# Linear attention on one Trainium2 core: log decays split into two rounded parts, running sums from rounded products

## The chip, the cores and the metric

The kernel runs on one core of one Trainium2 chip. The metric is device time in microseconds of one execution, as the median of several runs. The engines of the core are named as the profile names them: PE (TensorE matmul; PEld is its weight load), DVE (VectorE), ACT (ScalarE), POOL (GpSimd) and SP (SyncE, which issues DMAs).

## What is computed

The kernel is a two-layer backbone over 2048 latent and 256 context tokens of width 1024. The change concerns one part of the first layer, the bidirectional gated linear attention: 4 heads, key width 64, value width 128. Cut to what matters, the reference computes per direction:

```python
logits = jnp.einsum('bnzr,zrk->bnzk', r, gate_w) + gate_b
g = jax.nn.log_sigmoid(logits.astype(jnp.float32)) / GATE_TAU      # log decays
...
b = jnp.cumsum(gi, axis=-2)                                         # running sums in a chunk
b_last = b[..., -1:, :]
q_t = qi * jnp.exp(b)
k_t = ki * jnp.exp(-b)
att = jnp.where(mask, jnp.einsum('bhld,bhmd->bhlm', q_t, k_t), 0.0)
o = jnp.einsum('bhld,bhde->bhle', q_t, state) + jnp.einsum('bhlm,bhme->bhle', att, vi)
k_dec = ki * jnp.exp(b_last - b)
state = state * jnp.exp(b_last)[..., 0, :, None] + jnp.einsum('bhld,bhle->bhde', k_dec, vi)
```

All inputs are float32.

## The kernel before

The kernel goes through both layers in stages; the linear attention belongs to the stage `even_mix`, in which the latent attention (`even_attention`, heads in four pairs) is the main stream of PE and the linear attention (`gla`) is woven into it. The 2304 tokens are cut into 18 chunks of 128, and each chunk holds both directions side by side: a tile of 128 tokens x 512 columns is 4 heads x 2 directions x 64.

Per chunk, in `gla`:

- `logits` (L725): one rounded product of the low-rank gate gives 128x512 logits in PSUM; DVE makes G = min(logit, 0) (L733) and e = 2G - logit (L734), two tiles of 512 floats.
- `softplus` (L737): ACT makes e = ln(1 + exp(e)) in two passes (they are booked under the helper's line L106), then POOL makes G = G - e (L744). G is the log decay, still without the factor 1/16.
- `decays` (L752): PE makes `mid`, the running sums within a half chunk, as two products of a triangular 128x128 matrix `tri` with G (L759, one per direction, 256 columns), and `hs`, the sums over half chunks, as four products with G as weights and the two-column matrix `ind` (L763). Both are float32 products. ACT takes exponentials of hs into `fac` and of mid into `gqt` and `gkt` (L106); POOL multiplies two columns of fac (L768); DVE multiplies gqt and gkt by the queries and keys (L773).
- `within` (L790): PE forms scores (L799), DVE masks them (L802, two tiles, "gat" and "ge"), POOL adds the two (L804).
- `values` and `added` (L808, L818): PE multiplies the scores with the values (L813) and gkt with the values (L823); DVE takes them out of PSUM (L815, L824); POOL carries the state on (`scan`, L838 to L840), which only the second pass reads.
- `turn` (L777): PE transposes gqt and gkt (L785). A second pass over the chunks then reads the carried states.

The order of the work is set in three places. `gla` is a generator that yields names of places ("before", "middle", "after", "turn", "second"), and `even_attention` takes the next piece at these places between its own matmuls (L1130 scores, L1040 values; ACT takes exponentials into "apt", DVE adds them up into "acc", L1137). Hints (`issue_after`) bind pieces behind a given instruction. Within this, a scheduler of the framework puts the instructions of each engine into one order, in which the engine then executes them. In the order as compiled, a chunk's middle goes on PE: scores of the linear attention (L799), attention scores (L1130), L759, L763, sixteen L1040, L813 of the chunk before, L823 of this chunk, then attention again. On POOL: L804, L744 for the next chunk, L768, L838, then L839 and L840.

Tiles live in pools of named rings. G is in the ring "gG" (two buffers, 128x512 floats), which later also takes raw columns of the output weights (`load_unit`, L1245). e, the second masked score tile and the squares of the second pass share the ring "ge" with two buffers. All PSUM tiles of the linear attention share the ring "gl" with two banks.

Of the kernel before, what the change touches and what calls it, by code (L numbers as in the profile page):

```python
# [11 lines left out]
F32R = mybir.dt.float32r  # L12
AF = mybir.ActivationFunctionType
ALU = mybir.AluOpType
# [3 lines left out]
P = 128  # L18
# [70 lines left out]
class Kern:  # L89
# [589 lines left out]
    def gla(self, gp, gs, g1, gd, pp, tag, spare):  # L679

        nc = self.nc
        g = nc.gpsimd
        H = 4
        self.gQ = self.scr("gQ", (NT, P, 512), F32)
        self.gO = self.scr("gO", (NT, P, 512), F32)
        raw = self.tl(gs, [P, 512], "ge")
# [16 lines left out]
        low, us, logs, tiles, turned, scores, rows = {}, {}, {}, {}, {}, {}, {}  # L703

        def fetch(c):

# [7 lines left out]
        def low_rank(c):  # L714

            if c not in low:
                return
            u3 = low.pop(c)
            ps = bank()
            nc.tensor.transpose(ps[:96, :P], u3[:].rearrange("p n d -> p (n d)"), self.ident[:])  # L720
            r = rT[c % 2]
            nc.vector.tensor_copy(r[:96, :], ps[:96, :P])
            nc.vector.tensor_tensor(out=r[32:64, :], in0=ps[32:64, :P], in1=r[32:64, :], op=ALU.subtract)

        def logits(c):  # L725

            if c >= NT:
                return
            lg = bank()
            self.woven = nc.tensor.matmul(lg[:], rT[c % 2][:], gw[:], start=True, stop=True)  # L730
            G = self.tl(g1, [P, 512], "gG", bufs=2)
            e = self.tl(gs, [P, 512], "ge")
            nc.vector.tensor_scalar(out=G[:], in0=lg[:], scalar1=0.0, scalar2=None, op0=ALU.min)  # L733
            nc.vector.scalar_tensor_tensor(out=e[:], in0=G[:], scalar=2.0, in1=lg[:], op0=ALU.mult, op1=ALU.subtract)  # L734
            logs[c] = G, e

        def softplus(c):  # L737

            if c >= NT:
                return  # L740
            G, e = logs[c]
            self.act(e[:], e[:], AF.Exp)
            self.act(e[:], e[:], AF.Ln, bias=1.0)
            g.tensor_tensor(out=G[:], in0=G[:], in1=e[:], op=ALU.subtract)  # L744

        def inputs(c):

# [3 lines left out]

        def decays(c):  # L752

            u, G = us.pop(c), logs.pop(c)[0]
            gq, gk, gv = u[:, :256], u[:, 256:512], u[:, 512:1024]
            G4 = G[:].rearrange("p (h z d) -> p h z d", z=2, h=H)
            mid = bank()
            for z in range(2):
                nc.tensor.matmul(mid[:].rearrange("p (h z d) -> p h z d", z=2, h=H)[:, :, z, :], tri[:, z, :], G4[:, :, z, :], start=True, stop=True)  # L759
            hs = bank()  # L760
            hs4 = hs[:, : 2 * H].rearrange("p (h c) -> p h c", h=H)
            for h in range(H):
                self.woven = nc.tensor.matmul(hs4[:, h, :], G[:, h * P : h * P + P], ind[:], start=True, stop=True)  # L763
# [4 lines left out]
            g.tensor_tensor(out=f[:, :, 2], in0=f[:, :, 0], in1=f[:, :, 1], op=ALU.mult)  # L768
            qt = self.tl(g1, [P, 512], "gqt", bufs=1)
            kt = self.tl(g1, [P, 512], "gkt", bufs=1)  # L770
            for dst, src, sc in ((qt, gq, 1 / 16), (kt, gk, -1 / 16)):
                self.act(dst[:], mid[:], AF.Exp, scale=sc)
                nc.vector.tensor_tensor(out=z4(dst[:]), in0=z4(dst[:]),  # L773
                                        in1=src.rearrange("p (h d) -> p h d", h=H).unsqueeze(2).to_broadcast([P, H, 2, 64]), op=ALU.mult)
            tiles[c] = gv, f, qt, kt
# [14 lines left out]
        def within(c):  # L790

            qT, kT = turned.pop(c)
            at = self.tl(g1, [P, H, P], "gat", bufs=1)
            t2 = self.tl(gs, [P, H, P], "ge")
            two, mm = [bank(), bank()], None
            for h in range(H):
                for z in (1, 0):
                    with self.tc.issue_after(mm.ins) if mm else ExitStack():
                        mm = nc.tensor.matmul(two[z][:, h * P : h * P + P], kT[z * 64 : z * 64 + 64, h, :], qT[z * 64 : z * 64 + 64, h, :],  # L799
                                              start=True, stop=True)  # L800
            for ps, z, dst in ((two[0], 0, at), (two[1], 1, t2)):
                nc.vector.tensor_tensor(out=dst[:], in0=ps[:].rearrange("p (h t) -> p h t", h=H),  # L802
                                        in1=tri[:, 2 + z : 3 + z, :].to_broadcast([P, H, P]), op=ALU.mult)
            g.tensor_tensor(out=at[:], in0=at[:], in1=t2[:], op=ALU.add)  # L804
            scores[c] = at
            self.woven = mm
# [54 lines left out]
        def squares(c):  # L861

            oi = rows[c][1]
            sq = self.tl(gs, [P, 512], "ge")
# [33 lines left out]
        nc.vector.tensor_tensor(out=gw[64:97], in0=raw[64:97], in1=gw[64:97], op=ALU.subtract)  # L898
# [1042 lines left out]
```

## Time and profile before

| | |
|---|---|
| median of 3 runs | 3567.04 us (3567.01 to 3576.52) |
| profiled execution | 3570.04 us, span from first to last instruction 3568.3 us |
| granted TensorE clock, mean over the span | 0.990 |
| stage of the change | about 1150 to 1600 us of the span |
| ACT and DVE in that stage | 226.98 and 334.38 of 450 us busy |

The profile is one execution recorded by the hardware profiler. A row of a timeline gives start in the span, length, engine, source line, operation and tiles (out <- in, shapes); "x8" means eight such instructions merged, and the length then reaches from the first start to the last end. Square brackets give the idle time of the engine before the row and who ended it. A row of a group gives count, busy time and mean duration in ns. A row of a tile gives count, then smallest, median and largest duration in ns, then first and last start. Lengths of matmuls overlap: the next one starts before the last one has drained, so the distance of starts is the rate. A float32 product shows as two records, one for each pass.

### The profile page before, as it was taken

What the parts mean: (1) busy time and instruction counts of PE and PEld (TensorE: products, weight loads), DVE (VectorE), ACT (ScalarE), POOL (GpSimd) and SP (SyncE); (2) the same over time, 40 slices, a digit from 0 to 9 for tenths busy, and PEclk for the clock granted to TensorE, in tenths of its full rate; (3) what the DMA queues carried; (4) which work ended last, traced back from release to release, by engine and by line L of the source; (5) the groups of instructions that cost most, each with busy time, mean ns of one, the idle gap of its engine ahead of it and who ended that gap; (6) DMA issues with size and microseconds to landing.
All of it is one profiled execution on the core that took longest, in us unless ns stands there. A gap on an engine that the chain in (4) does not pass through costs nothing.

```text
span 3568.3 us, 53989 instructions
## 1 busy us (share of the span) xinstructions
PE 3472.6 (97%) x19604; PEld 2686.9 (75%) x19604; DVE 2341.2 (66%) x4624; ACT 1389.5 (39%) x2516; POOL 1275.0 (36%) x1411
## 2 busy tenths in 40 slices
PE   8999998999999999999999999999899999999899
PEld 6888987888896666665557878888688887555577
DVE  4677655888885777768874345455588784666732
ACT  5454552111113544546663124444322223555510
POOL 1333430100101333322212234333344443888763
PEclk9999999999999999999999999999999999999999
DMA  7555554222215242434526544445744447888672
GB/s 254 149 154 165 143 146 137 71 86 76 87 51 153 72 131 71 121 106 141 161 88 193 166 146 136 136 144 168 227 152 125 142 122 200 227 213 223 187 230 95
DMA packets 375868, 517.07 MB, mean 145 GB/s; under 512 B 34009, under 2 KB 253609, under 8 KB 369698
## 3 DMA queue, kind: packets, MB, share of 16 engines
q1 hardware_dynamic: 330914, 422.62, 41.3%
q0 software_dynamic: 22032, 63.00, 5.8%
q10 hardware_dynamic: 22656, 27.99, 2.2%
q8 instruction: 156, 2.56, 0.3%
q14 instruction: 110, 0.90, 0.1%
HBM read 334.17 MB, written 179.30 MB: 144 GB/s over the span
## 4 chain that ended last, share of the span: by engine, by line
PE 82%; DMA 6%; DVE 5%; ACT 2%; POOL 2%; issue 2%; SPq 1%; DVEq 0%; ACTq 0%; POOLq 0%
PE gm L129 10%; PE gm L130 10%; PE gm L131 10%; PE st L1130 9%; PE av L1040 7%; PE mx L660 4%; PE st L1587 2%; PE o L1621 2%; DMA wraw<-w_od 2%; PE pj L130 2%; PE pj L129 2%; PE pj L131 2%; PE st L131 2%; PE st L129 2%; PE st L130 2%
## 5 line engine op out<-in xcount | busy, mean ns | idle before, releaser
L661 DVE TENSOR_REDUCE mm<-mx 128x1 f32<-128x512 f32 (+1 forms) x656 | 388.4, 627 | 82.4 <-PE mx L660 75.3
L106 ACT ACTIVATE apt<-st 128x1024 f32<-128x1024 f32 (+1 forms) x296 | 300.3, 1015 | 304.9 <-PE st L1130 290.4
L1137 DVE TENSOR_TENSOR acc<-acc,apt 128x1024 f32<-128x1024 f32 x256 | 340.8, 1331 | 79.8 <-ACT apt L106 60.9
L1130 PE MATMUL st<-aq,akh 64*128 64x512 f32 x1728 | 312.0, 408 | 1.2 <-ACT apt L106 0.8
L1040 PE MATMUL av<-apt,av 128*64 128x512 f32 x1152 | 265.8, 598 | 0.0
L660 PE MATMUL mx<-mk,mq 96*128 96x512 f32 (+1 forms) x656 | 235.9, 373 | 1.0 <-DMA mq<-QC 0.6
L1746 DVE TENSOR_TENSOR opt<-st,tab 128x64 f32<-128x64 f32 (+10 forms) x576 | 144.2, 314 | 140.1 <-PE st L1588 63.9
L1627 POOL TENSOR_TENSOR oacc<-oacc,opt 128x576 f32<-128x576 f32 (+5 forms) x192 | 221.8, 1178 | 39.2 <-ACT rl L106 19.6
L1130 PE MATMUL st<-aq,akl 64*128 64x512 f32 (+1 forms) x1152 | 230.5, 390 | 0.0
L1130 PEld LDWEIGHTS st<-aq,akh 64*128 64x128 f32 x1728 | 152.8, 185 | 82.6 <-ACT apt L106 29.4
L106 ACT ACTIVATE u<-gm 128x352 f32<-128x352 f32 (+1 forms) x140 | 68.5, 497 | 368.3 <-PE gm L131 208.5
L1504 DVE CUSTOM_DVE_ANT_1 mx<-mx,mtab 128x217 f32<-128x217 f32 (+12 forms) x576 | 184.1, 338 | 39.9 <-PE mx L1498 30.6
L1040 PEld LDWEIGHTS av<-apt,av 128*64 128x64 f32 x1152 | 76.3, 136 | 135.2 <-issue 134.3
L106 ACT ACTIVATE opt<-opt 128x930 f32<-128x930 f32 (+8 forms) x130 | 104.3, 805 | 109.7 <-DVE opt L1746 106.4
L660 PEld LDWEIGHTS mx<-mk,mq 96*128 96x128 f32 x656 | 121.2, 188 | 13.7 <-DVE mm L661 1.6
L1130 PEld LDWEIGHTS st<-aq,akl 64*128 64x128 f32 (+1 forms) x1152 | 112.1, 184 | 22.9
L106 ACT ACTIVATE x<-px,modB,modA 128x128 f32<-128x128 f32 x272 | 99.5, 468 | 61.4 <-PE px L339 50.1
L129 PE MATMUL gm<-w1h,hhi 128*128 128x512 f32 x288 | 116.1, 403 | 7.3 <-ACT onat L106 7.3
L129 PE MATMUL gm<-w0h,hhi 128*128 128x512 f32 x288 | 115.3, 400 | 2.1 <-DVE hhi L351 2.1
L130 PE MATMUL gm<-w1l,hhi 128*128 128x512 f32 x288 | 114.7, 398 | 0.0
L210 POOL TENSOR_TENSOR oss<-oss,mhalf 128x8 f32<-128x8 f32 x68 | 112.4, 1653 | 5.1
L131 PE MATMUL gm<-w1h,hlo 128*128 128x512 f32 x288 | 113.9, 396 | 0.0
(506 smaller groups left out, 9716.9 us busy)
## 6 DMA issues: line engine op xcount, KB each, us to landing
q<-Q SPq DMA_DIRECT2D x48, 512.0 KB
H<-x ACTq DMA_DIRECT2D x36, 512.0 KB
adaw<-ada_w SPq DMA_DIRECT2D x64, 256.0 KB
x<-H SPq DMA_DIRECT2D x32, 512.0 KB
wraw<-w_od SPq DMA_DIRECT2D x64, 256.0 KB
K1t<-okt POOLq DMA_DIRECT2D x32, 512.0 KB, 7.7
kt<-K1t SPq DMA_DIRECT2D x32, 512.0 KB
mtab<-rpb_q SPq DMA_DIRECT2D x16, 899.0 KB
```

The costliest lines, as they stand in the source:

```text
L106: return self.nc.scalar.activation(out, in_, func, **kw)
L129: self.nc.tensor.matmul(out, lh(k), rh(k), start=start and j == 0, stop=False)
L130: self.nc.tensor.matmul(out, lh(k), rl(k), start=False, stop=False)
L131: yield self.nc.tensor.matmul(out, ll(k), rh(k), start=False, stop=stop and j == n - 1)
L660: mm = nc.tensor.matmul(ps[:, :w], q[:A_QK, (t % 6) * P : (t % 6) * P + P], k[:A_QK, k0 : k0 + w], start=True, stop=True)
L661: nc.vector.tensor_reduce(out=m[:, t, n : n + 1], in_=ps[:, :w], axis=AX.X, op=ALU.max)
L1040: mm = nc.tensor.matmul(O[j, nb][i * 64 : i * 64 + 64, :w], V[j, kt // TT][:, kt % TT, i * 64 : i * 64 + 64], pts[:, i, :w], start=n == 0, ...
L1130: mm = nc.tensor.matmul(ps[:, o // 64, :w], k[o : o + r, kb, kq], Q[o : o + r, qb, :w], start=m == 0, stop=m == 4)
L1137: added = nc.vector.tensor_tensor(out=acc[:, :, :w], in0=a[:, :, :w], in1=pts[:, :, :w], op=ALU.add)
L1504: nc.vector.tensor_tensor_reduce(out=s, in0=s, in1=tb[:, ri : ri + rn, ci : ci + cn], scale=1.0, scalar=-3e38, op0=ALU.add, op1=ALU.max, a ...
L1627: self.psum = nc.gpsimd.tensor_tensor(out=a, in0=a, in1=pts[:, :, a0 - r0 : a1 - r0, :], op=ALU.add)
L1746: bias = nc.vector.tensor_tensor(out=pt[:, d[0], d[1]], in0=ps[:, d[0], d[1]], in1=tabs[j][i][:, ri : ri + rn, ci : ci + cn], op=ALU.add)
```

## The change

G and e both come from the ring "ge", which gets three buffers. POOL, after making G, splits it: `hi` is G rounded to the rounded format (a copy), `lo` is G - hi, rounded. The two parts take the ring "gG". Each product of `decays` becomes two rounded products that add up in PSUM: L759 has 4 products per chunk where it had 2, L763 has 8 where it had 4. The constants `tri` (first two matrices) and `ind` are cast once by DVE. The diff, without the passing of the buffer count at other places of the ring:

```diff
         ind = self.tl(gp, [P, 2], "ind")
         nc.sync.dma_start(ind[:], self.i["halves"])
+        halves = self.tl(gp, [P, 2], "halves", F32R)
+        tr = self.tl(gp, [P, 2, P], "tri2", F32R)
...
-            G = self.tl(g1, [P, 512], "gG", bufs=2)
-            e = self.tl(gs, [P, 512], "ge")
-            nc.vector.tensor_scalar(out=G[:], in0=lg[:], scalar1=0.0, scalar2=None, op0=ALU.min)
-            nc.vector.scalar_tensor_tensor(out=e[:], in0=G[:], scalar=2.0, in1=lg[:], op0=ALU.mult, op1=ALU.subtract)
+            G, e = [self.tl(gs, [P, 512], "ge", bufs=3)[:] for _ in range(2)]
+            nc.vector.tensor_scalar(out=G, in0=lg[:], scalar1=0.0, scalar2=None, op0=ALU.min)
+            nc.vector.scalar_tensor_tensor(out=e, in0=G, scalar=2.0, in1=lg[:], op0=ALU.mult, op1=ALU.subtract)
...
-            self.act(e[:], e[:], AF.Exp)
-            self.act(e[:], e[:], AF.Ln, bias=1.0)
-            g.tensor_tensor(out=G[:], in0=G[:], in1=e[:], op=ALU.subtract)
+            self.act(e, e, AF.Exp)
+            self.act(e, e, AF.Ln, bias=1.0)
+            g.tensor_tensor(out=G, in0=G, in1=e, op=ALU.subtract)
+            hi, lo = parts[c] = [self.tl(g1, [P, 512], "gG", F32R, bufs=2)[:] for _ in range(2)]
+            g.tensor_copy(hi, G)
+            g.tensor_tensor(out=lo, in0=G, in1=hi, op=ALU.subtract)
...
             for z in range(2):
-                nc.tensor.matmul(mid[:].rearrange("p (h z d) -> p h z d", z=2, h=H)[:, :, z, :], tri[:, z, :], G4[:, :, z, :], start=True, stop=True)
+                for n, x in enumerate(pair):
+                    nc.tensor.matmul(z4(mid[:])[:, :, z, :], tr[:, z, :], z4(x)[:, :, z, :], start=n == 0, stop=n == 1)
...
             for h in range(H):
-                self.woven = nc.tensor.matmul(hs4[:, h, :], G[:, h * P : h * P + P], ind[:], start=True, stop=True)
+                for n, x in enumerate(pair):
+                    self.woven = nc.tensor.matmul(hs4[:, h, :], x[:, h * P : h * P + P], halves[:], start=n == 0, stop=n == 1)
...
         nc.vector.tensor_copy(gw[:97], raw[:97])
+        nc.vector.tensor_copy(tr[:], tri[:, :2, :])
+        nc.vector.tensor_copy(halves[:], ind[:])
```

The compiled order of the engines changes with it at a few places: on ACT the three exponentials into fac come ahead of the logarithm of e in nearly every chunk; on POOL L768 and L838 come ahead of the subtraction, the copy and the second subtraction; on SP one load of output weights and one of the next layer's weights move by a place or two.

More of the change, by code (lines that the diff above doesn't have):

```diff
@@ L685, in gla @@
         self.gO = self.scr("gO", (NT, P, 512), F32)
-        raw = self.tl(gs, [P, 512], "ge")
+        raw = self.tl(gs, [P, 512], "ge", bufs=3)
         nc.sync.dma_start(raw[:97], self.i["gate_w"])
@@ L702, in gla @@
         z4 = lambda a: a.rearrange("p (h z d) -> p h z d", z=2, h=H)
-        low, us, logs, tiles, turned, scores, rows = {}, {}, {}, {}, {}, {}, {}
+        low, us, logs, parts, tiles, turned, scores, rows = {}, {}, {}, {}, {}, {}, {}, {}
         def fetch(c):
@@ L752, in decays @@
         def decays(c):
-            u, G = us.pop(c), logs.pop(c)[0]
+            u, pair = us.pop(c), parts.pop(c)
+            del logs[c]
             gq, gk, gv = u[:, :256], u[:, 256:512], u[:, 512:1024]
-            G4 = G[:].rearrange("p (h z d) -> p h z d", z=2, h=H)
             mid = bank()
             for z in range(2):
-                nc.tensor.matmul(mid[:].rearrange("p (h z d) -> p h z d", z=2, h=H)[:, :, z, :], tri[:, z, :], G4[:, :, z, :], start=True, stop=True)
+                for n, x in enumerate(pair):
+                    nc.tensor.matmul(z4(mid[:])[:, :, z, :], tr[:, z, :], z4(x)[:, :, z, :], start=n == 0, stop=n == 1)
             hs = bank()
@@ L793, in within @@
             at = self.tl(g1, [P, H, P], "gat", bufs=1)
-            t2 = self.tl(gs, [P, H, P], "ge")
+            t2 = self.tl(gs, [P, H, P], "ge", bufs=3)
             two, mm = [bank(), bank()], None
@@ L863, in squares @@
             oi = rows[c][1]
-            sq = self.tl(gs, [P, 512], "ge")
+            sq = self.tl(gs, [P, 512], "ge", bufs=3)
             ss = self.tl(gs, [P, H], "gss")
```

## The prediction

> **What bounds the kernel now.** First the page: the share of each engine. Then the stage in which the changed lines run (1150 to 1600 us, the chunks of linear attention woven into the latent attention), as busy time in that stretch. Then the chain of waits over two and a half chunks.
>
> ```profile
> PE 3472.6 (97%) x19604; PEld 2686.9 (75%) x19604; DVE 2341.2 (66%) x4624; ACT 1389.5 (39%) x2516; POOL 1275.0 (36%) x1411
> ...
> 1150.00:1600.00 450.00, 448.14 (x3176) 287.69 (x3173) 334.38 (x347) 226.98 (x337) 155.28 (x130) 1.00 0.33 98
> ...
> by line: PE st L1130 41.2%; PE av L1040 29.9%; PE gl L813 5.4%; PE gl L759 5.4%; PE gl L799 4.5%; PE gl L763 3.9%; PE gl L785 3.4%; PE gl L823 3.3%; PE gl L956 1.4%; PE gl L720 0.8%; PE gl L730 0.8%
> ```
>
> PE is busy 448 of 450 us in this stage at the full granted clock (1.00), and the chain from 1240 to 1300 us is PE alone: L759 (running sums) has 5.4% of it and L763 (half-chunk sums) 3.9%. So PE time removed here shortens the kernel, as long as nothing else becomes late. What could become late is seen in one chunk. This is the timeline of all engines from 1269 to 1277 us (start, length, engine, line), thinned to the rows used below:
>
> ```profile
> 1266.62 2.56 DVE L1137 TENSOR_TENSOR acc<-acc,apt 128x1024 f32<-128x1024 f32 x2
> ...
> 1269.69 0.68 DVE L802 TENSOR_TENSOR gat<-gl,tri 128x512 f32<-128x512 f32 x1
> 1269.91 0.73 PEld L759 LDWEIGHTS gl<-gG,tri 128*128 128x128 f32 x4 [0.35 <-DVE ge L802]
> ...
> 1270.29 3.43 DVE L1137 TENSOR_TENSOR acc<-acc,apt 128x1024 f32<-128x1024 f32 x2
> 1270.45 2.18 POOL L804 TENSOR_TENSOR gat<-gat,ge 128x512 f32<-128x512 f32 x1 [4.24 <-DVE gat L802]
> 1270.67 1.08 PEld L763 LDWEIGHTS gl<-ind,gG 128*128 128x128 f32 x8
> 1270.88 0.95 PE L763 MATMUL gl<-ind,gG 128*128 128x2 f32 x8
> ...
> 1272.43 0.64 ACT L106 ACTIVATE ge<-ge 128x512 f32<-128x512 f32 x1
> ...
> 1272.95 0.41 ACT L106 ACTIVATE fac<-gl 64x8 f32<-64x8 f32 x3
> ...
> 1273.15 1.71 POOL L744 TENSOR_TENSOR gG<-gG,ge 128x512 f32<-128x512 f32 x1 [0.51 <-ACT ge L106]
> ...
> 1273.64 1.76 DVE L773 TENSOR_TENSOR gqt<-gqt,gu 128x512 f32<-128x512 f32 x1
> ...
> 1274.81 0.65 POOL L768 TENSOR_TENSOR fac<-fac 128x4 f32<-128x4 f32 x1
> 1275.32 0.68 DVE L773 TENSOR_TENSOR gkt<-gkt,gu 128x512 f32<-128x512 f32 x1
> 1275.35 0.97 PEld L813 LDWEIGHTS gl<-gu,gat 128*128 128x128 f32 x8 [0.81 <-POOL gG L744]
> ...
> 1275.54 1.37 POOL L838 TENSOR_TENSOR gsf<-gsf,fac 64x512 f32<-64x512 f32 x1
> 1276.23 0.97 PEld L823 LDWEIGHTS gl<-gu,gkt 128*128 128x128 f32 x8
> ```
>
> Two things are to be seen. PE needs gkt at L823, at 1276.23; DVE finishes gkt at 1275.32 + 0.68 = 1276.00. That is 0.23 us ahead, and in the next chunk the gap is the same, 0.22 us, although PE had to break off between L813 and L823 there:
>
> ```profile
> 1298.74 0.68 DVE L773 TENSOR_TENSOR gkt<-gkt,gu 128x512 f32<-128x512 f32 x1
> ...
> 1298.89 0.75 PEld L813 LDWEIGHTS gl<-gu,gat 128*128 128x128 f32 x6
> 1299.64 0.97 PEld L823 LDWEIGHTS gl<-gu,gkt 128*128 128x128 f32 x8
> ```
>
> So about 0.23 us is the time from DVE's end to PE's load, and **DVE is already level with PE** at this point. Second, DVE and POOL wait for each other. Two sums L1137 take 2.56 us without POOL beside them and 3.43 us with L804 beside them. L744 was issued at 1273.15, gqt at 1273.64, and gqt ends at 1275.40, 0.54 us after L744 (1274.86). L838 was issued at 1275.54, behind gkt (1275.32); gkt takes its plain 0.68 and L838 ends 0.91 after it. I read this as: of a DVE and a POOL operation that both read SBUF, the one issued first runs, the other waits for its end; then gqt or gkt takes 0.55, L838 0.91, and L744 1.13 (1274.86 less 1273.73, where the second sum ends).
>
> By the Trainium skill, "SBUF — State Buffer", section "Who interferes with whom", a VectorE instruction with two SBUF inputs and a GpSimd instruction that reads SBUF exclude each other for the whole instruction, in order of issue. The rows above agree (gqt 1.76 us behind L744, gkt 0.68 ahead of L838). The rule speaks against this change, which gives GpSimd two more such operations per chunk.
>
> **The change, part by part.** *Running sums.* L759 runs 36 products as 72 records, two passes each, and L763 72 products as 144. A rounded product is one record (L1130: 4 head pairs x 72 key tiles x 6 = 1728). The nearest rounded product of 256 columns with full weights is L1491:
>
> ```profile
> L759 PE MATMUL gl<-gG,tri x72: 379/379/483, 1151.4 to 1572.6; 128*128 128x256 f32 x72
> ...
> L763 PEld LDWEIGHTS gl<-ind,gG x144: 190/192/192, 1152.2 to 1573.5; 128*128 128x128 f32 x144
> L763 PE MATMUL gl<-ind,gG x144: 167/251/251, 1152.4 to 1573.5; 128*128 128x2 f32 x144
> ...
> L1130 PE MATMUL st<-aq,akh 64*128 64x512 f32 x1728 | 312.0, 408 | 1.2 <-ACT apt L106 0.8
> ...
> L1130 PEld LDWEIGHTS st<-aq,akh 64*128 64x128 f32 x1728 | 152.8, 185 | 82.6 <-ACT apt L106 29.4
> ...
> 2559.80 0.28 PE L1491 MATMUL mx<-mk,mz 128*128 128x256 f32 x1
> 2559.92 0.33 PE L1498 MATMUL mx<-mk,mz 128*128 128x352 f32 x1
> ...
> 2560.36 0.28 PE L1491 MATMUL mx<-mk,mz 128*128 128x256 f32 x1
> 2560.47 0.39 PE L131 MATMUL gm<-w2h,hlo 128*128 128x512 f32 x1
> ```
>
> Now: first load of L759 at 1269.91, first matmul of L763 at 1270.88, 0.97 us; less one load of 0.11 that nothing covers, that is four passes of 0.215. Then: four rounded passes of 0.11 to 0.12 (from L1491's start to the next matmul: 0.12 and 0.11), 0.46 to 0.47 us. PE gains 0.39 us per chunk, 18 x 0.39 = **7.0 us** at most.
>
> The Trainium skill, "FP8 and Floating Point Precision", section "TensorE Precision Notes", counts four passes for a true fp32 product; two rounded ones would then be half of it, 0.43 per chunk and 7.7 us in all. The trace has two records of double length per product, which comes to the same; by the row of L1491 the sum is 7.0.
>
> *Half-chunk sums.* Eight passes of two columns before and after. Eight loads start within 1.08 less the last one's 0.19, 0.89 us, so each costs about 0.11, which is the load of 128 weights and not the two columns. A rounded load of 128 weights lasts as long as these (L1130 185 ns, L763 190 to 192 ns), which excludes a gain. I take 0; the upper bound is 0.12 per pass as in L1491, 18 x 8 x 0.01 = 1.4 us.
>
> *Split on POOL.* Added per chunk: a copy and a subtraction, 128x512. Rows: L744 and a copy of 512 elements:
>
> ```profile
> L744 POOL TENSOR_TENSOR gG<-gG,ge 128x512 f32<-128x512 f32 x17 | 29.0, 1706 | 16.5 <-ACT ge L106 16.5
> ...
> L835 POOL COPY gsf<-D 64x512 f32<-64x512 f32 x1 | 0.6, 605 | 2.3 <-DVE D L824 2.3
> ```
>
> 0.6 + 1.1 to 1.7 us, so about 18 x 2 = 36 us of POOL, which has 155 of 450 us busy. Who waits for the split, and who waits at the start and near the two new casts of the constants:
>
> ```profile
> 1293.24 0.73 PEld L759 LDWEIGHTS gl<-gG,tri 128*128 128x128 f32 x4 [0.38 <-DVE ge L802]
> ...
> 1287.62 0.69 DVE L733 TENSOR_SCALAR gG<-gl 128x512 f32<-128x512 f32 x1
> ...
> 1145.16 1.88 POOL L744 TENSOR_TENSOR gG<-gG,ge 128x512 f32<-128x512 f32 x1 [15.61 <-DMA aq<-QC]
> ...
> 1148.87 3.88 DVE L1137 TENSOR_TENSOR acc<-acc,apt 128x1024 f32<-128x1024 f32 x3 [2.98 <-ACT apt L106]
> ...
> 1126.96 0.69 DVE L898 TENSOR_TENSOR gw<-ge,gw 33x512 fp32r<-33x512 f32 x1 [8.51 <-DMA gw<-gw]
> ```
>
> In the chunk above the split ends near 1279 (below); the next chunk's L759 wants it at 1293.24, so the longer path costs nothing. The parts have one pair of buffers, free when this chunk's L763 ends (1271.83), before POOL comes to write them. G now lives in the ring of three "ge" buffers, so DVE's next L733 waits for the split's end: 1279 against 1287.62. POOL's L839 and L840 come some 2 us later; their results are read only after the last chunk. If the cover of 8 to 14 us were gone, PE would wait at L759 for what is missing. At the start the second L734 waits for the first split, 1147.04 + 0.6 + 1.7 = 1149.3, and DVE's sums queue behind it; the first of them began at 1148.87, after 2.98 us of idling. With L734's 0.69 they come 1.1 us later; No row tells whether PE feels that once; I take 0, at most 1.1.
>
> *What moves.* In the compiled streams ACT does the three fac exponentials ahead of the logarithm of ge (L106) in nearly every chunk, and POOL does fac (L768) and gsf x fac (L838) ahead of the subtraction that was L744 and of the split. Elsewhere a few DMA issues on SP swap neighbours (one w_out load now waits for the last L763, as the second one did already; one w_od load comes earlier): 0. The two small casts of the constants on DVE lie in front of its 8.51 us wait for a DMA: 0.
>
> **The sum.** DVE's order and the start of its burst don't change, since what feeds it comes before L759. In the chunk above: fac's exponentials end 0.52 earlier, at 1272.84, and POOL issues L768 near 1272.9. The second sum L1137 has been running since L804 ended (1272.63) and ends at 1273.72. Then L768 (0.1), gqt (0.55, to 1274.37), L838 (issued 1273.9, before gkt; 0.91, to 1275.28), gkt (0.55, to 1275.83); behind it the former L744 (1.13), the copy (0.6) and the last subtraction (1.1 to 1.7), to about 1279. L823 can load at 1275.83 + 0.23 = 1276.06. PE would be there at 1276.23 - 0.39 = 1275.84 and waits. **Gain 0.17 of the 0.39.** How many chunks are like this:
>
> ```profile
> L773 DVE TENSOR_TENSOR gqt<-gqt,gu 128x512 f32<-128x512 f32 x18 | 27.3, 1517 | 1.3 <-ACT gqt L106 1.3
> L773 DVE TENSOR_TENSOR gkt<-gkt,gu 128x512 f32<-128x512 f32 x18 | 14.1, 786 | 0.0
> ```
>
> With n long gqt of 1.76 and the rest 0.68, 27.3 gives n = 14. In the other 4 gqt is not held up, and I count all of the 0.39. 14 x 0.17 + 4 x 0.39 = 2.4 + 1.6 = **4.0 us**. The profiled execution took 3570.04 us (span 3568.3); 3566.0 after. The median of the three runs is 3.0 below it, 3567.04, so 3563.0 in its terms.
>
> **The rivals.** *All of the gain arrives*: L768 or L838 takes less room than I gave, gkt ends before 1275.6. For it: POOL's subtraction no longer stands before gqt. Against it: L838 takes its place. 7.0 us: 3560.
>
> *The gain is eaten whole*: gkt ends at 1276.0 or a little later, since ACT's fac comes later than I place it or the split's operations hold up the sums L1137 near 1280. For it: DVE is busy without a gap from 1266.62 to 1276.00. 1.6 us gain down to 5 us loss: 3565.5 to 3572.
>
> *Slower*: POOL gets ahead of DVE by one operation. If L768 is issued before the second sum has the port, L838 is issued before gqt, and the subtraction (former L744) before gkt: from 1273.72, 0.91 + 0.55 + 1.13 + 0.55 = 1276.86 for gkt, L823 at 1277.09, 0.86 late. 14 x 0.86 = 12.0, less the four free chunks' 1.6, is 10.4 lost: 3577.5 (3578.6 with the 1.1 us at the start). It decides at 1272.63, the end of L804: fac's exponentials miss it by 0.2 us in this chunk.
>
> *The change doesn't do what it says*: rounded passes of this strided form (4 x 64) or of two columns are no faster than now. Then PE gains nothing: 3567.
>
> **How the numbers follow.** Forecast 0.49 (3561 to 3565.5), all of the gain 0.16, eaten whole 0.15, no faster passes 0.04, slower 0.16. The range 3557 to 3574 takes in all but the slower rival and no more: from 3560 less 3 for the spread of executions to 3572 and 2 more; one of the three runs shown lay 9.5 above the others (3576.52). 0.3% is 10.7 us (about what a measurement of this kernel can tell from no change). Faster than 3556.3 would need more than PE has to give here: 0.05. Slower than 3577.7 is most of the slower rival, since a chunk that loses 0.86 here has its later sums held up as well: 0.14. Within: 0.81.
>
> **What would show it.** Right: records of the running sums 0.11 to 0.12 apart and of the half-chunk sums 0.11; 36 us more POOL in the stage; gqt at about 0.7 to 0.75 and gkt at 1.4 to 1.5 where they now read 1.76 and 0.68; L823's weights waiting 0.2 us for DVE; from one L759 to the next 0.2 less than now (23.33 in this chunk). Wrong: gkt behind POOL's subtraction (L823 waiting 1 us), or a wait of PE on the split itself ahead of the running sums, or rounded two-column passes above 0.12.

## The result, and the profile after

| | before | after |
|---|---|---|
| median | 3568.80 us (3567.01 to 3576.52, 5 runs) | 3588.06 us (3581.76 to 3592.82, 5 runs) |
| ratio | | 1.0045, 95% interval 1.0034 to 1.0055 |
| profiled execution | 3570.04 us, span 3568.3 | 3592.56 us, span 3590.5 |

The kernel became slower by 0.45%, beyond the predicted range of 3557 to 3574 us. The ratio, here and below, is the one on record with its interval; it isn't the quotient of the two medians, which is 1.0054 here. Line numbers are now those of the changed kernel: L764 is the running sums (L759 before), L769 the half-chunk sums (763), L774 fac (768), L779 gqt and gkt (773), L810 the addition into gat (804), L844 gsf x fac on 64 partitions (838), L819 and L829 the products with the scores and with gkt (813, 823), L1145 DVE's sums (1137), L745 the subtraction G - e (744), L747 the copy, L748 the second subtraction. Experiments move these numbers, by nine lines at most.

First the engines' shares of the page, and then the stage from 1150 to 1600 us as in the prediction (columns: length, then busy time and count of PE, PEld, DVE, ACT and POOL, granted clock, DMA share, GB/s).

```profile
PE 3478.4 (97%) x19604; PEld 2688.9 (75%) x19604; DVE 2347.7 (65%) x4626; ACT 1390.7 (39%) x2516; POOL 1315.4 (37%) x1447
```

```profile
1150.00:1600.00 450.00, 432.82 (x3089) 275.53 (x3086) 334.24 (x336) 222.36 (x330) 189.56 (x165) 1.00 0.30 95
```

PE, busy 448.14 of these 450 us before, is now busy 432.82 at the same granted clock of 1.00: it waits 15 us more. The waits of PE in this stretch say for whom (total, times, longest):

```profile
PE gl L829 <- DVE gkt L779: 15.3, 14, 1.1
```

In 14 chunks PE waits about 1.1 us at L829 for gkt. Before, no such row was there. The groups of DVE's two multiplications (busy, mean ns of one):

```profile
L779 DVE TENSOR_TENSOR gkt<-gkt,gu 128x512 f32<-128x512 f32 x18 | 42.1, 2338 | 0.0
...
L779 DVE TENSOR_TENSOR gqt<-gqt,gu 128x512 f32<-128x512 f32 x18 | 12.6, 699 | 0.9 <-ACT gqt L106 0.9
```

gqt, 1517 ns before, is short; gkt, 786 ns before, is three times as long. One chunk shows why. This is the timeline of all engines from the first running sum to L829 (start, length), thinned:

```profile
1302.01 0.54 PEld L764 LDWEIGHTS gl<-gG,tri 128*128 128x128 f32 x4 [0.39 <-DVE ge L808]
...
1302.47 3.43 DVE L1145 TENSOR_TENSOR acc<-acc,apt 128x1024 f32<-128x1024 f32 x2
1302.61 0.97 PEld L769 LDWEIGHTS gl<-halves,gG 128*128 128x128 f32 x8
1302.61 1.05 PE L769 MATMUL gl<-halves,gG 128*128 128x2 f32 x8
1302.64 2.18 POOL L810 TENSOR_TENSOR gat<-gat,ge 128x512 f32<-128x512 f32 x1 [6.19 <-DVE gat L808]
...
1305.00 0.96 POOL L774 TENSOR_TENSOR fac<-fac 128x4 f32<-128x4 f32 x1 [0.18 <-ACT fac L106]
...
1305.83 0.68 DVE L779 TENSOR_TENSOR gqt<-gqt,gu 128x512 f32<-128x512 f32 x1
1306.04 1.37 POOL L844 TENSOR_TENSOR gsf<-gsf,fac 64x512 f32<-64x512 f32 x1
...
1306.43 2.75 DVE L779 TENSOR_TENSOR gkt<-gkt,gu 128x512 f32<-128x512 f32 x1
...
1307.37 1.26 POOL L745 TENSOR_TENSOR ge<-ge,ge 128x512 f32<-128x512 f32 x1
1308.69 0.96 POOL L747 CAST gG<-ge 128x512 fp32r<-128x512 f32 x1
...
1309.40 0.97 PEld L829 LDWEIGHTS gl<-gu,gkt 128*128 128x128 f32 x8 [1.25 <-issue]
...
1309.73 1.27 POOL L748 TENSOR_TENSOR gG<-ge,gG 128x512 fp32r<-128x512 f32 x1
```

gkt is issued at 1306.43 while L844 runs (to 1307.41). By the prediction's reading it should come next. It ends at 1309.18, which is 1.77 us after L844 but 0.55 us after L745 (1308.63), an operation issued 0.94 us *behind* gkt. In all 14 chunks the distance to L745's end is 0.55 us. L829 starts 7.39 us after the first running sum here; in the prediction's two chunks that was 6.32 (1276.23 less 1269.91) and 6.40.

A yardstick used below is the row of the running sums' products, which gives the start of its first record, in chunk 1, and of its last, the fourth of chunk 18: 1151.4 to 1572.6 before, 421.2 us apart. After:

```profile
L764 PE MATMUL gl<-gG,tri x72: 277/282/392, 1157.1 to 1590.5; 128*128 128x256 f32 x72
```

433.4 us, 12.2 more. (The four records of chunk 18 themselves moved 0.3 us closer; from the first record of chunk 1 to the first of chunk 18 it is 420.5 and 432.9.) Of the 22.2 us between the two spans, 12.2 arise in this stretch, 5.7 ahead of its first row (1157.1 less 1151.4, see the start, below) and 4.3 behind its last: 2000.0 us follow it here and 1995.7 before, and in all thirteen profiled executions of this case 1993.8 to 2000.0.

### The profile page after: what moved, and what is told of

Same layout as the page of the kernel before. It is cut to its first block, busy times and chain, and to the rows that moved or that the text cites. A ratio compares the mean times of both kernels' runs of the same rounds, so it can differ in the third digit from the quotient of the medians.

```text
span 3590.5 us, 54054 instructions
## 1 busy us (share of the span) xinstructions
PE 3478.4 (97%) x19604; PEld 2688.9 (75%) x19604; DVE 2347.7 (65%) x4626; ACT 1390.7 (39%) x2516; POOL 1315.4 (37%) x1447
## 5 line engine op out<-in xcount | busy, mean ns | idle before, releaser
L1145 DVE TENSOR_TENSOR acc<-acc,apt 128x1024 f32<-128x1024 f32 x256 | 340.0, 1328 | 78.5 <-ACT apt L106 58.4
L1048 PE MATMUL av<-apt,av 128*64 128x512 f32 x1152 | 265.8, 598 | 0.0
L1048 PEld LDWEIGHTS av<-apt,av 128*64 128x64 f32 x1152 | 76.3, 136 | 135.2 <-issue 134.3
```

Source lines behind the costliest of these rows:

```text
L1048: mm = nc.tensor.matmul(O[j, nb][i * 64 : i * 64 + 64, :w], V[j, kt // TT][:, kt % TT, i * 64 : i * 64 + 64], pts[:, i, :w], start=n == 0, ...
L1145: added = nc.vector.tensor_tensor(out=acc[:, :, :w], in0=a[:, :, :w], in1=pts[:, :, :w], op=ALU.add)
```

## The experiments

The theory after the result: the order on GpSimd alone makes the loss. GpSimd now runs the 64-partition multiplication (844) and the 128-partition subtraction (745) back to back, and VectorE's multiplication with two SBUF inputs isn't let in between. Rivals: the split's own work on GpSimd, or the prediction's plain rule (the one issued first runs) at other instants. What the expectations call the port is what GpSimd and VectorE exclude each other from. Each table row gives the median, the ratio to the kernel before, and the distance between the first and last record of the running sums (421.2 in the kernel before). The ratios are to executions of the kernel before that were taken with each experiment, whose medians were 3571.45 to 3575.00 us. Two of e_twice's ten executions took 6019 and 17865 us; they are in its median and not in its ratio, and nothing on record says why.

| run | median us (runs) | ratio [95%] | first to last record |
|---|---|---|---|
| b_order | 3585.29 (5) | 1.0037 [1.0024, 1.0049] | 434.8 |
| e_hionly | 3586.94 (4) | 1.0041 [1.0027, 1.0055] | 433.4 |
| e_late | 3572.48 (11) | 1.0001 [0.9992, 1.0010] | 421.9 |
| e_full | 3569.85 (11) | 0.9992 [0.9982, 1.0001] | 418.0 |
| e_twice | 3569.33 (10) | 0.9991 [0.9981, 1.0001] | 418.0 |
| e_up | 3567.23 (10) | 0.9994 [0.9984, 1.0003] | 418.5 |
| e_low | 3569.21 (10) | 0.9992 [0.9982, 1.0003] | 418.5 |
| e_96 | 3587.98 (6) | 1.0033 [1.0020, 1.0045] | 436.4 |
| e_casts | 3586.76 (5) | 1.0038 [1.0025, 1.0050] | 435.3 |
| e_gw | 3564.07 (11) | 0.9979 [0.9970, 0.9988] | 418.0 |
| b_gw | 3570.06 (11) | 0.9998 [0.9988, 1.0007] | 422.7 |

**The order alone (b_order).** The kernel before, with the subtraction placed behind gsf x fac:

```diff
+        def differ(c):
+            if c >= NT:
+                return
+            G, e = logs[c]
             g.tensor_tensor(out=G[:], in0=G[:], in1=e[:], op=ALU.subtract)
...
-                eng.tensor_tensor(out=N[sl], in0=S[sl], in1=f[sl, :, 2:3].to_broadcast([n, H, P]), op=ALU.mult)
+                self.scanned = eng.tensor_tensor(out=N[sl], in0=S[sl], in1=f[sl, :, 2:3].to_broadcast([n, H, P]), op=ALU.mult)
...
             if c < NT:
                 added(c)
+                with self.tc.issue_after(self.scanned.ins):
+                    differ(c + 1)
```

> The kernel before, with one thing moved: POOL does the subtraction of the next chunk (L744) behind the carried state's multiplication (L838) and not ahead of fac (L768), as in the changed kernel. No split, no rounded product; the order of PE, DVE, ACT and SP is that of before. Theory (order on POOL): L838 and L744 run one right behind the other and DVE's gkt (L773) waits for both, so gkt ends near +7.1 us after the first load of L759 where it ended at +6.1, L823 starts at +7.3, about 1.0 us lost in each of 14 chunks: 3568.8 + 14 = about 3583. Rival (the added POOL work of the split, or the rounded products, make the loss): nothing of either is here, so no difference from before, 3568.8.

The same picture, in the old kernel (timeline of b_order; L750 is its subtraction):

```profile
1300.78 1.36 POOL L844 TENSOR_TENSOR gsf<-gsf,fac 64x512 f32<-64x512 f32 x1
1301.17 2.75 DVE L779 TENSOR_TENSOR gkt<-gkt,gu 128x512 f32<-128x512 f32 x1
1302.11 1.26 POOL L750 TENSOR_TENSOR gG<-gG,ge 128x512 f32<-128x512 f32 x1
...
1304.14 0.97 PEld L829 LDWEIGHTS gl<-gu,gkt 128*128 128x128 f32 x8 [1.00 <-issue]
```

gkt is 2.75 us long, L829 is late, and the stretch takes 434.8 us without any rounded product or split. The order is enough for the loss.

**No split, order as changed (e_hionly).** The subtraction writes the rounded part, which is used twice; the small part is left out of the computation.

```diff
-            g.tensor_tensor(out=G, in0=G, in1=e, op=ALU.subtract)
-            hi, lo = parts[c] = [self.tl(g1, [P, 512], "gG", F32R, bufs=2)[:] for _ in range(2)]
-            g.tensor_copy(hi, G)
-            g.tensor_tensor(out=lo, in0=G, in1=hi, op=ALU.subtract)
+            hi = self.tl(g1, [P, 512], "gG", F32R, bufs=2)[:]
+            parts[c] = hi, hi
+            g.tensor_tensor(out=hi, in0=G, in1=e, op=ALU.subtract)
```

> The changed kernel without the split: GpSimd's subtraction (745) writes the rounded decays itself and both products use that one part, so the copy (747) and the second subtraction (748) are gone and the small part is left out of the computation. The order of what remains on GpSimd is that of the changed kernel. Theory A (what costs is that the subtraction stands right behind the 64-partition multiplication 844, and VectorE's gkt waits for both): gkt still ends 6.9 to 7.2 us behind the first running sum and 829 starts at +7.2 to +7.4 in the 14 chunks, 3580 to 3590 us, ratio 1.003 to 1.005. Rival S (the split's own 2.2 us of GpSimd time per chunk is the cost): gkt ends near +5.9, 829 at +6.1, 3566 to 3572 us.

The group of gkt in e_hionly:

```profile
L778 DVE TENSOR_TENSOR gkt<-gkt,gu 128x512 f32<-128x512 f32 x18 | 42.1, 2340 | 0.0
```

As in the changed kernel (2338 ns), and the stretch is 433.4 us as well. The split's work on GpSimd costs nothing that can be seen; rival S is out.

**The subtraction and split later (e_late).** The changed kernel, with L745, L747 and L748 moved behind the last operation of the scan (846):

```diff
+        def split(c):
+            if c >= NT:
+                return
+            G, e = logs[c]
             g.tensor_tensor(out=G, in0=G, in1=e, op=ALU.subtract)
...
-                last.tensor_tensor(out=d[sl], in0=S[sl], in1=f[sl, :, 0:1].to_broadcast([n, H, P]), op=ALU.mult)
+                self.scanned = last.tensor_tensor(out=d[sl], in0=S[sl], in1=f[sl, :, 0:1].to_broadcast([n, H, P]), op=ALU.mult)
...
+                with self.tc.issue_after(self.scanned.ins):
+                    split(c + 1)
```

> The changed kernel, with the subtraction and the split on POOL behind the whole carrying of the state (after L840), so that gkt meets only L838. Every other engine keeps the order of the changed kernel; the split's work is all there. Theory (order on POOL): gkt ends near +5.9 to +6.0, L823 starts near +6.1 to +6.2, against +7.3 in the changed kernel; 14 x 1.15 = 16 us faster than it, 3572, and about 0.2 us per chunk less than before from one L759 to the next. Rival (the split's work or the rounded products cost the time): stays near 3588, with PE waiting elsewhere in the chunk.

gkt is back at 1387 ns in the mean, and the load of L829 comes 5.93 to 6.18 us after the first running sum in every chunk but the first (5.04). Yet the stretch takes 421.9 us, where 0.2 us less per chunk than before, as expected, would be near 418. The trace shows a new place for the same wait (timeline of e_late; 852 is the 64-partition end of the scan, 751 the subtraction; the DVE row merges two sums):

```profile
1186.88 1.04 POOL L852 TENSOR_TENSOR D<-gsf,fac 64x512 f32<-64x512 f32 x1
1187.04 4.77 DVE L1154 TENSOR_TENSOR acc<-acc,apt 128x1024 f32<-128x1024 f32 x2 [1.66 <-ACT apt L106]
1187.88 1.29 POOL L751 TENSOR_TENSOR ge<-ge,ge 128x512 f32<-128x512 f32 x1
```

The first of the two sums was issued at 1187.04, behind 852 and ahead of 751, and ends at 1190.25, 2.33 us after 852 and 1.08 us after 751. In 13 chunks it is the same, to 0.01 us. This wait alone doesn't cost the stretch its gain: e_twice, e_up and e_low, below, have it too, in 12 chunks each, at 418.0 to 418.5 us. But here the split's two operations fall beside the same sums as well. In one chunk four sums take 8.31 us, where in e_full the same four take 6.29, and PE then waits for DVE's L978, which comes right behind them (the second row is of the waits from 1150 to 1600 us):

```profile
1210.19 8.31 DVE L1154 TENSOR_TENSOR acc<-acc,apt 128x1024 f32<-128x1024 f32 x4 [1.66 <-ACT apt L106]
...
PE gl L732 <- DVE rl L978: 3.2, 5, 0.7
```

e_full has no such row. These 3.2 us are most of the 3.9 between 421.9 and e_full's 418.0; no run separates the split's part of the delay from the subtraction's.

**All 128 partitions (e_full).** The changed kernel, its order untouched, with the forward scan's multiplication over all 128 partitions. The upper half is thrown away.

```diff
+            w = slice(0, P) if name == "gsf" else sl
             if S is None:
-                eng.tensor_copy(N[sl], d[sl])
+                eng.tensor_copy(N[w], d[w])
...
-                eng.tensor_tensor(out=N[sl], in0=S[sl], in1=f[sl, :, 2:3].to_broadcast([n, H, P]), op=ALU.mult)
+                eng.tensor_tensor(out=N[w], in0=S[w], in1=f[w, :, 2:3].to_broadcast([w.stop - w.start, H, P]), op=ALU.mult)
```

> The changed kernel, with the forward carrying's multiplication (L838) on all 128 partitions instead of the 64 that are needed; the rest of the order is the same, the subtraction still comes right behind it. Theory A (an operation on 64 partitions leaves half of POOL idle, the next one starts there before the first has ended, and the port is never free in between): now gkt gets in between the two, ends near +6.0, and the time falls by 14 x 1.1 = 15 us to about 3573. Theory B (POOL keeps the port whenever its next operation is ready): gkt still waits for both, ends near +7.1, 3588.

The timeline of e_full (845 is the multiplication):

```profile
1293.85 0.53 PEld L764 LDWEIGHTS gl<-gG,tri 128*128 128x128 f32 x4 [0.40 <-DVE ge L808]
1294.45 0.97 PEld L769 LDWEIGHTS gl<-halves,gG 128*128 128x128 f32 x8
...
1297.67 0.68 DVE L779 TENSOR_TENSOR gqt<-gqt,gu 128x512 f32<-128x512 f32 x1
1297.88 1.36 POOL L845 TENSOR_TENSOR gsf<-gsf,fac 128x512 f32<-128x512 f32 x1
1298.27 1.53 DVE L779 TENSOR_TENSOR gkt<-gkt,gu 128x512 f32<-128x512 f32 x1
...
1299.21 1.72 POOL L745 TENSOR_TENSOR ge<-ge,ge 128x512 f32<-128x512 f32 x1
...
1300.02 0.97 PEld L829 LDWEIGHTS gl<-gu,gkt 128*128 128x128 f32 x8
```

L845 is no longer or shorter than on 64 partitions (1.36 us), and the subtraction is again issued just before its end. But gkt now ends 0.55 us after 845, at 1299.80, and it is the subtraction that waits (1.72 us, for 1.26). The load of L829 starts at +6.17, and no wait of PE for gkt of over 0.15 us is left. A multiplication twice as wide, half of it useless, takes away the whole loss: 418.0 us.

**Two halves (e_twice).** Is it enough that all partitions are touched? The multiplication as two instructions:

```diff
-                eng.tensor_copy(N[sl], d[sl])
+                w = slice(0, P) if name == "gsf" else sl
+                eng.tensor_copy(N[w], d[w])
...
-                eng.tensor_tensor(out=N[sl], in0=S[sl], in1=f[sl, :, 2:3].to_broadcast([n, H, P]), op=ALU.mult)
+                for w in [slice(0, 64), slice(64, P)] if name == "gsf" else [sl]:
+                    eng.tensor_tensor(out=N[w], in0=S[w], in1=f[w, :, 2:3].to_broadcast([w.stop - w.start, H, P]), op=ALU.mult)
```

> The changed kernel with the forward scan's multiplication (844) written as two instructions, partitions 0 to 63 and 64 to 127, with the rest of GpSimd's order as it is. All 128 partitions are covered, as in the kernel that took the loss away, but by two instructions with 64 each. Theory A (an instruction on 64 partitions lets the next one start on the free half, so that VectorE finds no gap in the chain): the two run one over the other or end to end, the subtraction 745 follows without a gap, and gkt ends only after 745 has ended, at +7.0 or later; 3584 to 3605 us. Rival B (VectorE gets its turn at any end of a GpSimd instruction, and the full multiplication only moved the instant): gkt ends before 745 starts, near +6.8 or earlier; 3570 to 3582 us.

```profile
1297.73 2.82 POOL L846 TENSOR_TENSOR gsf<-gsf,fac 64x512 f32<-64x512 f32 x2
1298.12 1.53 DVE L779 TENSOR_TENSOR gkt<-gkt,gu 128x512 f32<-128x512 f32 x1
...
1332.41 1.28 POOL L745 TENSOR_TENSOR ge<-ge,ge 128x512 f32<-128x512 f32 x1
...
1334.33 1.28 POOL L847 TENSOR_TENSOR gsf<-gsf,D 64x512 f32<-64x512 f32 x1
1335.28 4.66 DVE L1147 TENSOR_TENSOR acc<-acc,apt 128x1024 f32<-128x1024 f32 x2 [1.67 <-ACT apt L106]
1335.57 1.29 POOL L748 TENSOR_TENSOR gG<-ge,gG 128x512 fp32r<-128x512 f32 x1
```

Theory A as I had written it missed: the first half ends at 1299.09, the second is issued at 1299.15, and gkt ends at 1299.64, 0.55 us behind the first half and 0.91 ahead of the second's end (1300.55): it was served between the two. So not every instruction behind one on 64 partitions keeps VectorE out. In the same run the lower rows show one that does: behind 847 (64 partitions, to 1335.61) the second subtraction (128) starts at 1335.57, 0.04 us before that end, and the sum issued at 1335.28 ends at 1337.94, 1.08 us after the *subtraction*. What differs is the size of the second instruction and the partition that it starts at (0, not 64), and that it was issued 0.04 us before the end of the first and not 0.06 us after it.

**Which half, and how much of it (e_up, e_low, e_96).** The subtraction 745 in two pieces; 844 stays on 0 to 63. e_up takes 64 to 127 first, e_low 0 to 63 first, e_96 0 to 95 first.

```diff
-            g.tensor_tensor(out=G, in0=G, in1=e, op=ALU.subtract)
+            for w in (slice(64, P), slice(0, 64)):
+                g.tensor_tensor(out=G[w], in0=G[w], in1=e[w], op=ALU.subtract)
```

> The changed kernel with GpSimd's subtraction (745) written as two instructions of 64 partitions, the upper half (64 to 127) first; it stands right behind the multiplication 844 on partitions 0 to 63. Theory I (the next instruction takes hold of the half that 844 leaves idle, so VectorE, which needs both halves, finds one of them taken when 844 ends): gkt is served only after the first piece has ended, 1.7 us or more after 844's end, ends at +6.9 or later, and the time is 3582 to 3595 us. Rival N (an instruction on 128 partitions behind one on 64 keeps VectorE out, one on 64 does not, whichever half): gkt ends 0.55 us after 844, at about +5.9, and the time is 3566 to 3574 us.

> The same with the lower half (0 to 63, the half that 844 uses) first, the upper half second. Theory I: the first piece can take hold of nothing while 844 runs, gkt ends 0.55 us after 844, at about +5.9, 829 starts at about +6.1, and the time is 3566 to 3574 us. Rival N: the same as with the upper half first, gkt 0.55 us after 844 in both. Rival Q (GpSimd keeps the port over any chain whose next instruction was issued before the end of one on 64 partitions): gkt only after the first piece, at +6.9 or later, in both, 3582 to 3595 us.

> The changed kernel with the subtraction (745) as two instructions, partitions 0 to 95 and then 96 to 127, behind the multiplication 844 on 0 to 63. The pieces on 0 to 63 and on 64 to 127 both let VectorE in; the first was issued 0.03 us before 844 ended, but touches nothing that 844 leaves free, the second was issued only 0.06 us after it. This piece starts at partition 0 and reaches 32 partitions into the free half. Theory I (an instruction that is issued before the end of one on 64 partitions and reaches into the free half holds the port): the piece is issued 0.03 us before 844 ends, gkt ends only after it, 1.7 us or more behind 844, 829 starts at +7.2 or later, and the first running sum of the last chunk comes 432 to 436 us after that of the first; 3580 to 3592 us. Rival N (only an instruction on all 128 partitions does so): gkt ends 0.55 us behind 844, 418 to 419 us, 3566 to 3572 us.

Timelines of e_up, e_low and e_96 (845 is the multiplication on 64 partitions, 746 the two pieces in one row):

```profile
1294.91 1.37 POOL L845 TENSOR_TENSOR gsf<-gsf,fac 64x512 f32<-64x512 f32 x1
1295.30 1.53 DVE L780 TENSOR_TENSOR gkt<-gkt,gu 128x512 f32<-128x512 f32 x1
...
1296.34 2.96 POOL L746 TENSOR_TENSOR ge<-ge,ge 64x512 f32<-64x512 f32 x2
```

```profile
1296.68 1.37 POOL L845 TENSOR_TENSOR gsf<-gsf,fac 64x512 f32<-64x512 f32 x1
1297.07 1.53 DVE L780 TENSOR_TENSOR gkt<-gkt,gu 128x512 f32<-128x512 f32 x1
...
1298.01 3.04 POOL L746 TENSOR_TENSOR ge<-ge,ge 64x512 f32<-64x512 f32 x2
```

```profile
1303.85 1.36 POOL L845 TENSOR_TENSOR gsf<-gsf,fac 64x512 f32<-64x512 f32 x1
1304.23 2.75 DVE L780 TENSOR_TENSOR gkt<-gkt,gu 128x512 f32<-128x512 f32 x1
...
1305.17 2.94 POOL L746 TENSOR_TENSOR ge<-ge,ge 96x512 f32<-96x512 f32 x2
```

e_low and e_96 differ in nothing but the piece's end, 64 or 96. In both runs the first piece is issued before 845 ends (1298.01 against 1298.05; 1305.17 against 1305.21). The one that stays within 845's half lets gkt in (1.53 us). The one that reaches 32 partitions into the free half keeps it out (2.75 us, in all 14 chunks), and with it the loss is back in full: 436.4 us. That is theory I's forecast for these two, and it rules out N (only 128 partitions) and Q (any instruction that is issued early). In e_up theory I missed: the piece on the upper half was issued 0.06 us *after* 845's end, as in e_twice, and gkt got in. Why GpSimd issues a piece that starts at partition 64 that much later than one that starts at 0 isn't shown.

**The start (e_casts, e_gw, b_gw).** The first running sum came 5.7 us later than before. Part of it is a wait of PE for the gate weights `gw`, whose last row comes by a transfer that SyncE issues behind a queue of attention loads, at 1124.85 us before and at 1128.08 after. (The bracket names rT, the product's other input; VectorE makes it right behind gw, for which it idled 8.5 us before and 10.2 after.) The first gate product, before, after and in e_full:

```profile
1128.02 0.50 PE L730 MATMUL gl<-gw,rT 98*128 98x512 f32 x1 [1.32 <-DVE rT L723]
```

```profile
1131.32 0.80 PE L732 MATMUL gl<-gw,rT 98*128 98x512 f32 x1 [2.98 <-DVE rT L725]
```

```profile
1128.78 0.53 PE L732 MATMUL gl<-gw,rT 98*128 98x512 f32 x1 [3.43 <-DVE rT L725]
```

Another part is the granted clock behind this wait. In the changed kernel's trace it is 0.50 for 6.8 us:

```profile
1130.60:1137.40 6.80, 6.08 (x26) 4.48 (x28) 6.04 (x8) 1.49 (x2) 0.46 (x1) 0.50 0.02 4
```

From the first gate product to the first running sum it takes 25.8 us there. In the five profiles with the full clock at this place (before, b_order, b_gw, e_up, e_gw) it takes 23.4, and in the other seven, with a clock of 0.50 for 3.4 us, 24.8 to 25.0. So of the 5.7 us, 2.4 are the halved clock, 1.7 the longer wait (2.98 less 1.32), and 1.6 come from further ahead.

e_casts puts the two casts of the constants behind the gate weights' subtraction:

```diff
-        nc.vector.tensor_copy(tr[:], tri[:, :2, :])
-        nc.vector.tensor_copy(halves[:], ind[:])
...
+        with self.tc.issue_after(split_bias.ins):
+            nc.vector.tensor_copy(tr[:], tri[:, :2, :])
+            nc.vector.tensor_copy(halves[:], ind[:])
```

> The changed kernel, with the two casts of the constants behind the gate weights' subtraction (former L898) instead of ahead of it. It is about the 4 us that the profile of the changed kernel lost before the first L759 (about 1130 us), with the clock at one half for 6.8 us there. If the casts make that loss: the first L759 starts 4 us earlier, the clock stays whole, 3584. If it is scatter of the DMA that the gate weights wait for: no difference from 3588 beyond the scatter, and the loss comes and goes in these executions too.

The wait stays (2.96 us): the casts aren't its cause. e_gw is e_full with the transfer on GpSimd's queue, and b_gw is the kernel before with that edit alone:

```diff
-        nc.sync.dma_start(gw[97:98].bitcast(F32), gw[96:97].bitcast(F32))
+        nc.gpsimd.dma_start(gw[97:98].bitcast(F32), gw[96:97].bitcast(F32))
```

> The changed kernel with the multiplication 844 on all 128 partitions, and with the one-row transfer gw<-gw issued by GpSimd in place of SyncE. Theory G (the 2.4 to 3.9 us lost at 1120 to 1131 us are the wait of the gate weights for this transfer behind SyncE's queue of attention loads): it is issued some 5 us or more earlier, TensorE's delay against the kernel before does not grow between 1115 and 1140 us, and the time is 2 to 4 us under that of the full multiplication alone: 3564 to 3568 us, ratio 0.998 to 0.999. Rival H (the gate weights wait for something else that is late, such as 897's bank or the earlier loads themselves): the delay still grows by 2 to 4 us there and the time is 3568 to 3572 us.

> The kernel before with nothing changed but the one-row transfer gw<-gw, issued by GpSimd in place of SyncE. It tells how much of the gain of the changed kernel with both edits is the transfer's. If the transfer alone: 3563 to 3567 us, ratio 0.998. If it matters only where SyncE's queue is as late as in the changed kernel: no change, ratio 0.999 to 1.001.

In e_gw the transfer goes out at once and the product follows PE's earlier work:

```profile
1119.99 0.58 POOL L906 DMA_DIRECT2D gw<-gw  x1 [3.04 <-DVE halves L905]
...
1128.79 0.50 PE L732 MATMUL gl<-gw,rT 98*128 98x512 f32 x1
```

The wait is gone, as theory G said, and the clock behind it stays whole. e_gw is faster than both kernels, 0.9979 [0.9970, 0.9988]; b_gw, whose trace has no wait there either, gains nothing measurable (0.9998). But the wait isn't the change's for certain: it is 2.4 to 3.4 us in seven profiled executions of kernels with the change, and 1.6 in e_up and e_96, which have the same start; 0.9 and 1.3 in b_order and before. Nor does its length alone tell the clock: behind 1.6 us it stayed whole in e_up and was halved in e_96. Whether the queue is later by the change or by chance stays open; the 4.1 us of wait and clock, of the 22.2 between the two profiled spans, depend on it. Nor is e_gw's lead over e_full settled, since their intervals meet.

## Why the prediction was wrong

The step that failed is the fourth in the sum: "L838 (issued 1273.9, before gkt; 0.91, to 1275.28), gkt (0.55, to 1275.83); behind it the former L744". Everything ahead of gkt came as written, and so did its duration once it was served. What failed is *who is served next*. I read from the trace of before that the operation issued first runs and the other waits for its end. The Trainium skill, "SBUF — State Buffer", section "Who interferes with whom", says the same. Both hold in e_full, e_twice and e_low, where gkt ends 0.55 us behind the multiplication or its first half. They don't hold where L838, on 64 partitions, is followed at once by an instruction that reaches beyond them: the subtraction, issued later than gkt, ran first in 14 chunks of the changed kernel. The pair of L838 and L744 back to back was not in the trace of before, where L744 stood in front.

- *PE's gain* was right for the running sums. From the first load of the running sums to the first matmul of the half-chunk sums it is 0.60 us (1302.61 less 1302.01) where it was 0.97: 0.37 less, for a forecast of 0.39. The half-chunk sums' eight loads start within 0.78 us (0.97 less 0.19) where they took 0.88, 0.10 less, where I took 0 and held a gain to be excluded. The two don't add up: from the first load of the running sums to the first load of the product that follows (L1040 before, L1048 after) it is 1.85 us in each chunk before and 1.46 to 1.58 after, 1.51 in the median, a gain of 0.34. In e_full the stretch is 3.2 us shorter than before; forecast 4.0.
- *gqt* at 0.68 and 1.53 for gkt (e_full) are within 0.03 us of the forecast's "0.7 to 0.75" and "1.4 to 1.5". L829 at +6.17 there is the forecast's 6.15 (1276.06 less 1269.91).
- *gkt* was 2.75 us and L829 waited 14 times, 15.3 us in all. 421.2 less 4.0 plus 15.3 is 432.5; measured 433.4.
- *The split on POOL*: 0.61 us for the copy where DVE leaves it alone (e_full, e_twice) or 0.96, and 1.27 for the second subtraction. POOL's 189.56 us in the stage, for 155.28, are the 36 us within 2. Its cost of nothing was right (e_hionly).
- *The start*: I allowed 0 to 1.1 us for DVE's first sums. The first running sum came 5.7 us later instead, by PE's wait for the gate weights, the halved clock behind it and differences further ahead.
- *The rival "slower"* named the right place (gkt behind the former L744), and its "0.86 late" for 14 chunks stands against 1.1. But its route was wrong: it had POOL get ahead at L768 by 0.2 us, and gave that 0.16. POOL's and DVE's order of issue was that of the forecast; no luck of instants was needed, since 844 and 745 in a row did it in all 14 chunks in which gkt was waiting.

## What to carry to other kernels

Where instructions of GpSimd and VectorE exclude each other, as here, and VectorE is on the critical path, look at what follows a GpSimd instruction on part of the partitions: if the next one reaches into the partitions left free, VectorE can wait for both. Covering all partitions with a throw-away upper half cost nothing here and won the loss back. And a scheduler that moves one instruction on an engine that is busy for 36% of the span, as GpSimd was here, can cost more than all that the change set out to gain, so read the new order pair by pair, also for pairs that the old trace doesn't hold.

## What the runs showed of the hardware

- A GpSimd multiplication of 512 elements takes 1.36 us beside DVE on 64 (after, L844) and on 128 partitions (e_full, L845) alike.
- In these pairs a GpSimd instruction that starts at partition 0 is issued 0.03 to 0.05 us before the last one ends where it waits for nothing of it. Behind one on partitions 0 to 63, an instruction that starts at 0 and reaches beyond 63 then keeps a waiting VectorE operation with two SBUF inputs out until it has ended itself: gkt ended 0.55 us behind the second in 14 of 14 chunks each of after, b_order, e_hionly, e_casts and e_96, and DVE's sums 1.08 us behind it in the 13 of e_late and the 12 each of e_twice, e_up and e_low. Behind one on 128 (e_full) or within 0 to 63 (e_low), it ended 0.55 us behind the first, 14 of 14 each.
- The Trainium skill, "GPSIMD Engine Reference", section "2.1 Instruction dispatch", states that each of GpSimd's cores serves 16 partitions and goes on to the next instruction as soon as its own share is done. That cores without a share in 844 begin the next instruction and so keep VectorE out over its end would give what e_96 and e_low show. This is argued, not shown: the pieces that start at partition 64, issued 0.06 us after the end, are not explained by it, and no run shows the cores one by one.
- A load of 128 rounded weights lasts 0.19 us in the record, as a float32 one does (L769 after, L763 before), but eight of them start within 0.78 us where the float32 ones took 0.88.
